# Moving the split rows and split weights of a float32r transformer kernel to other byte offsets

## The chip, the cores and the metric

The kernel runs on one core of one Trainium2 chip. The metric is the device time of one execution in microseconds, the median of the runs; lower is better. Before the change it was 2332.92 us (two runs, 2332.77 to 2333.07).

## What is computed

A two-layer decoder trunk in float32: model width 2048, 16 heads of 128, 256 tokens behind 16 learned prefix tokens (272 positions), feed-forward width 8192.

```python
h = concat([meta, x])                                   # 272 positions
for layer in range(2):
    a = rms_norm(h, norm_attn[layer])
    if layer == 0:
        q, k, v, f_logit = split(a @ fox_w_in)          # 3 * 2048 + 16 columns
        o = forgetting_attention(q, k, v, cumsum(log_sigmoid(f_logit + b)))
        h = h + o @ fox_w_o
    else:
        k, v = split(rms_norm(h, kv_norm) @ w_kv)
        o = stick_breaking_attention(a @ sb_w_q, k, v)
        h = h + o @ sb_w_o
    h = h + square(relu(rms_norm(h, norm_mlp[layer]) @ w_up[layer])) @ w_down[layer]
return rms_norm(h, final_norm)[:, 16:]
```

Every weight is read once: 406 MB over the execution.

## The kernel before

Activations stand feature-major: a tensor of 2048 features is 16 chunks of 128 partitions, each chunk a row of 272 positions (layer 0 and the K/V projection, which need the prefix tokens) or 256 (the rest of layer 1).

For accuracy each float32 operand is split into two float32r parts, hi (the rounded value) and lo (what is left of it). A product of weights and activations is then made of three: hi weights by hi rows, hi weights by lo rows, lo weights by hi rows. They are accumulated in one PSUM bank.

**Rows.** The class `Split` (line 117) holds both parts of an activation tensor in one tile of the pool `xs`, which has two buffers. A chunk has `XROW` = 576 floats of 4 bytes, a pitch of 2,304 bytes or 9 x 256. The hi part begins at float `XHI` = 16 (64 bytes), the lo part right behind it, n floats on, where n is 272 or 256. `self.both` is the two of them as one run of 2n. ScalarE writes the hi part and VectorE the lo part: in `split_chunk` (line 127) after a residual, in `put_split` (line 354) after an attention, and in the MLP's evacuation (lines 496 to 500).

**Weights.** `gemm_group` (line 178) makes 512 output features of one projection, as four accumulators of 128 features. It walks four blocks `kb` of four input chunks each. A block arrives as two `raw` tiles of 128 x 1024 over the SP queue (line 202); of each, ScalarE makes `whi` (line 213) and VectorE `wlo` (line 214), tiles of the pool `wspl` with four buffers for each of the two names. These are [128, 2, 512] floats: two input chunks with a pitch of 2,048 bytes. A load of PE takes 128 of the 512 columns.

**Products.** All of them are issued through `gemm_matmul` on line 172, in an order written out by hand and pinned by dependencies, except in the first group. In layer 0 and the K/V projection (`pairs` false) an input chunk and an accumulator cost three matmuls of 272 columns: hi rows by `whi`, lo rows by `whi`, hi rows by `wlo`. In the rest of layer 1 (`pairs` true) they cost two: `sp.both` by `whi`, 512 columns in one go, so that the two parts land in the two halves of a bank, and hi rows by `wlo`, 256 columns. The evacuation then adds the two halves (`total`, line 254, or two calls of line 252). In the last group of all, accumulator 3 is made with the three separate products (`apart`).

There are 12 groups for Q, K and V of layer 0, 4 for its output projection, 32 for its MLP (4 slices of 4 up and 4 down groups), 4 for the Q of layer 1, 8 for K and V, 4 for its output projection and 32 for its MLP. `uid` numbers them from 1 to 96; the attention between them works on other pools. The order of the pools in memory is `const`, `wraw`, `align` (a pad of 128 bytes), `wspl`, `xs`, `tmp`, `att`.

The labels of the row tiles are `a0` (rows for Q, K, V of layer 0), `o0` (attention output), `m0` (MLP input), `u0_0` to `u0_3` (the four slices of the hidden layer), `a1` (rows for Q of layer 1), `kv` (rows for K and V), `o1`, `m1` and `u1_0` to `u1_3`. The output is collected in `ob`, the last tile of `xs`.

Of the kernel before, what the change touches and what calls it, by code (L numbers as in the profile page):

```python
# [9 lines left out]
F32 = mybir.dt.float32  # L10
F32R = mybir.dt.float32r
# [4 lines left out]
P = 128  # L16
D = 2048
NC = D // P
# [4 lines left out]
BIG = 1.0e30  # L23
QSCALE = 1.0 / math.sqrt(P)
N_FF = 4
XROW = 576
XHI = 16

G_A0, G_M0, G_KV, G_A1, G_M1, G_FIN = range(6)

# [2 lines left out]
def yoco_kernel(ctx: ExitStack, tc: tile.TileContext, hT_in, gains, b_f, w_f, w_qkv0, w_o0, w_up, w_dn,  # L33
                w_kv, w_q1, w_o1, outT):
    nc = tc.nc
# [5 lines left out]
    wspl = ctx.enter_context(tc.tile_pool(name="wspl", bufs=4))  # L41
    xs = ctx.enter_context(tc.tile_pool(name="xs", bufs=2))
# [74 lines left out]
    class Split:  # L117


        def __init__(self, label, t0):  # L120
            n = T - t0
            self.t0 = t0
            rows = xs.tile([P, NC, XROW], F32R, tag="x", name=f"x_{label}")
            self.hi, self.lo = rows[:, :, XHI:XHI + n], rows[:, :, XHI + n:XHI + 2 * n]
            self.both = rows[:, :, XHI:XHI + 2 * n]

    def split_chunk(sp, gi, c):

# [41 lines left out]
    def gemm_matmul(*args, **kw):  # L170

        ins = nc.tensor.matmul(*args, **kw).ins  # L172
        if queued and pinned[0]:
            tc.add_manual_dep(ins, queued[0].name, mybir.DependencyInfo(mybir.DependencyClass.NoSync,
                                                                        mybir.DependencyReason.DATA))
        queued[:] = [ins]

    def gemm_group(wblk, sp, t0, evac, before={}, after={}, load_x=None, pairs=False, apart=()):

        uid[0] += 1
        u = uid[0]
        accs = [pacc.tile([P, 512], F32, tag="acc", name=f"acc_{u}_{m}") for m in range(4)]
        n = T - t0
        for kb in range(4):
            src_w = wblk[kb].rearrange("p (k c) -> p k c", k=4)
            if kb in before:  # L190
                before[kb]()
            piece = 1 if load_x is not None and kb < 2 else 2
            raws = [wraw.tile([P, 2, 512], F32, tag="raw", name=f"raw_{u}_{kb}_{hf}") for hf in range(2)]
            for k0 in range(0, 4, piece):
                if load_x is not None:
                    load_x(range(4 * kb + k0, 4 * kb + k0 + piece))
                if load_x is not None and kb == k0 == 0:

                    for c0 in (0, 256):
                        nc.scalar.dma_start(raws[0][:, 0, c0:c0 + 256], src_w[:, 0, c0:c0 + 256])  # L200
                else:
                    nc.sync.dma_start(raws[k0 // 2][:, k0 % 2:k0 % 2 + piece], src_w[:, k0:k0 + piece])
            parts = []
            for hf in range(2):
                whi = wspl.tile([P, 2, 512], F32R, tag="whi", name=f"whi_{u}_{kb}_{hf}")
                wlo = wspl.tile([P, 2, 512], F32R, tag="wlo", name=f"wlo_{u}_{kb}_{hf}")
                boxes = [(o, piece, 0, 512) for o in range(0, 2, piece)]
                if load_x is not None and kb == hf == 0:
                    boxes[:1] = [(0, 1, 0, 256), (0, 1, 256, 512)]
                for o, no, c0, c1 in boxes:  # L210
                    src = raws[hf][:, o:o + no, c0:c1]
                    hp, lp = whi[:, o:o + no, c0:c1], wlo[:, o:o + no, c0:c1]
                    on_act = nc.scalar.activation(hp, src, AF.Copy)  # L213
                    on_dve = nc.vector.tensor_tensor(out=lp, in0=src, in1=hp.bitcast(F32), op=ALU.subtract)  # L214
                parts.append((whi, wlo))
            if kb in after:
                with tc.issue_after(on_act.ins), tc.issue_after(on_dve.ins):
                    after[kb]()


            if load_x is not None and kb == 0:
                runs = [([kc], range(4)) for kc in range(4)]
            elif kb in (0, 3):
                runs = [(range(4), [m]) for m in range(4)]
            else:
                runs = [(range(2 * hf, 2 * hf + 2), range(4)) for hf in range(2)]
            pinned[0] = load_x is None
            for kcs, ms in runs:
                paired = [m for m in ms if pairs and m not in apart]
                single = [m for m in ms if m not in paired]  # L230
                for kc in kcs:
                    for m in paired:
                        gemm_matmul(accs[m], parts[kc // 2][0][:, kc % 2, m * P:(m + 1) * P], sp.both[:, 4 * kb + kc],
                                    start=kb == kc == 0, stop=False)
                for kc in kcs:
                    for m in paired:
                        gemm_matmul(accs[m][:, :n], parts[kc // 2][1][:, kc % 2, m * P:(m + 1) * P],
                                    sp.hi[:, 4 * kb + kc], start=False, stop=kb == kc == 3)
                for m in single:
                    for kc in kcs:  # L240
                        wh, wl = (w[:, kc % 2, m * P:(m + 1) * P] for w in parts[kc // 2])
                        hi, lo = sp.hi[:, 4 * kb + kc], sp.lo[:, 4 * kb + kc]
                        gemm_matmul(accs[m][:, :n], wh, hi, start=kb == kc == 0, stop=False)
                        gemm_matmul(accs[m][:, :n], wh, lo, start=False, stop=False)
                        gemm_matmul(accs[m][:, :n], wl, hi, start=False, stop=kb == kc == 3)
                if kb == 3:
                    for m in ms:
                        evac(m, [accs[m][:, :n]] + ([accs[m][:, n:]] if m in paired else []))
# [18 lines left out]
    def load_x(chunks):  # L267
        c0, n = chunks[0], len(chunks)
        nc.sync.dma_start(hT[:, c0:c0 + n, :], hT_in[:, c0:c0 + n, :])
        if c0 == 0:  # L270
            nc.sync.dma_start(g_sb, gains)
        for c in chunks:
            split_chunk(xa, G_A0, c)
# [86 lines left out]
    for g in range(4):  # L360
# [11 lines left out]
        if g == 0:  # L372

            gemm_group(w_qkv0[0], xa, 0, lambda m, acc, qT=qT: nc.scalar.copy(qT[:, m, :], acc[0]),
                       after={kb: (lambda kb=kb: first_norm(kb)) for kb in range(4)}, load_x=load_x)
            gate_products()
            box["rstd"] = norm.finish()
            for m in range(4):
                evac_q(m, [qT[:, m, :]])
            forget_gates(box["rstd"])  # L380
        else:
            gemm_group(w_qkv0[3 * g], xa, 0, evac_q)
# [4 lines left out]
        def decays(j):  # L387

            for i, (o, n) in enumerate(((0, 144), (144, T))):
                nc.vector.scalar_tensor_tensor(out=s[:, j, o:o + n], in0=fk[:, j, :n],  # L390
                                               scalar=fq_sb[:, i, 4 * g + j:4 * g + j + 1],
                                               in1=maskA[:, o:o + n], op0=ALU.subtract, op1=ALU.add)

        gemm_group(w_qkv0[3 * g + 1], xa, 0, lambda m, acc: evac_kv(m, acc, kT),
                   after={j: (lambda j=j: decays(j)) for j in range(4)})

# [255 lines left out]
    a, y, t, rs = (fin[:, i, :] for i in range(4))  # L652
# [9 lines left out]
    for i in range(2):  # L662
# [2 lines left out]
            nc.tensor.matmul(pr[:, b * P:(b + 1) * P], rs[:, b:b + 1].to_broadcast([P, P]), ident,  # L665
                             start=True, stop=True)
        prs.append(pr[:, :S])
    ob = xs.tile([P, NC, XROW], F32, tag="x", name="ob")
    pr_sb = tmp.tile([P, T], F32, tag="relu", name="pr_sb")[:, :S]
    nc.scalar.copy(pr_sb, prs[1])  # L670
    for c, n in [(12, 1), (13, 1), (14, 1), (15, 1), (0, 2), (2, 2), (4, 2), (6, 2)]:
# [62 lines left out]
```

## Time and profile before

| | |
|---|---|
| median of the runs | 2332.92 us |
| the profiled execution | 2332.09 us |
| its span, first to last instruction | 2330.3 us |
| mean granted TensorE clock | 0.998 |
| HBM traffic | 407.29 MB read, 176 GB/s over the span |

The profile gives for each engine its busy time and number of instructions. PE is TensorE's matmuls and PEld its weight loads, which overlap them; DVE is VectorE, ACT ScalarE. A line of a group of instructions has the source line, the engine, the operation, output and inputs by their names in the program, the shape, the count, the busy time in us and the mean of one record in ns, and then the idle time in front of them. Records of matmuls overlap, since matmuls are pipelined: two that follow each other are better compared by their starts than by their lengths. The view by stretches gives the busy time of every engine between two points of time.

### The profile page before, as it was taken

The page shows a single profiled execution, that of the slowest core. Times are in us where ns is not written, and L with a number is a line of the kernel's source. Part 1 is how long each engine was busy: PE and PEld are TensorE (multiplying, and loading weights), DVE is VectorE, ACT ScalarE, POOL GpSimd, SP SyncE. Part 2 cuts the span into 40 slices and gives each one's busy share as a digit, 9 for nine tenths or more (in the row PEclk, how much of TensorE's full clock was granted, in tenths as well). Part 3 has the DMA queues.
Part 4 walks back from the last instruction along what each step waited for, and adds up shares of the span by engine and source line. Part 5 has one row for each costly group of instructions (what it writes and reads, how often), then busy time and mean ns, then how long its engine had stood idle before and what let it go on. Part 6 is the DMA issues. An engine that isn't in the chain of part 4 may idle for free.

```text
span 2330.3 us, 39954 instructions
## 1 busy us (share of the span) xinstructions
PE 2319.3 (100%) x16486; PEld 2200.1 (94%) x16486; DVE 1350.6 (58%) x1923; ACT 1064.8 (46%) x1477; POOL 38.9 (2%) x58
## 2 busy tenths in 40 slices
PE   9999999999999999999999999999999999999998
PEld 9999999999999999999998999988888888888887
DVE  7665555654454455445566555566665665655665
ACT  6434344543344344334455444455543543543553
POOL 1000000000000000000000000000000000000000
PEclk9999999999999999999999999999999999999999
DMA  6544545455545555555556444446556556555553
GB/s 233 172 155 163 169 158 171 166 185 173 180 168 185 176 174 180 172 182 172 181 175 198 160 145 145 145 163 199 184 190 198 186 187 199 185 191 195 185 198 128
DMA packets 116630, 412.00 MB, mean 177 GB/s; under 512 B 13264, under 2 KB 16736, under 8 KB 116448
## 3 DMA queue, kind: packets, MB, share of 16 engines
q1 hardware_dynamic: 114560, 406.29, 52.4%
q10 hardware_dynamic: 1888, 3.16, 0.4%
q8 instruction: 129, 2.11, 0.4%
q14 instruction: 53, 0.43, 0.1%
HBM read 407.29 MB, written 2.11 MB: 176 GB/s over the span
## 4 chain that ended last, share of the span: by engine, by line
PE 99%; DVE 0%; ACT 0%; issue 0%; DVEq 0%; ACTq 0%
PE acc L172 96%; PE ps L402 0%; PE pza L581 0%; PE pv L335 0%; PE po L464 0%; PE po L620 0%; PE idle L60 0%; PE pzb L582 0%; PE po L621 0%; PE po L465 0%; PE po L622 0%; DVE ob L676 0%; PE pf L301 0%; PE pf L302 0%; PE pta L597 0%; PE pta L596 0%
## 5 line engine op out<-in xcount | busy, mean ns | idle before, releaser
L214 DVE TENSOR_TENSOR wlo<-raw,whi 128x1024 fp32r<-128x1024 f32 (+1 forms) x773 | 931.7, 1217 | 752.6 <-ACT whi L213 751.7
L213 ACT ACTIVATE whi<-raw 128x1024 fp32r<-128x1024 f32 (+1 forms) x773 | 799.2, 1050 | 960.4 <-PE acc L172 939.9
L172 PE MATMUL acc<-x_u,whi 128*128 128x272 f32 (+2 forms) x3088 | 650.8, 322 | 0.0
L172 PE MATMUL acc<-x_m,whi 128*128 128x272 f32 (+1 forms) x3072 | 649.2, 323 | 0.0
L172 PEld LDWEIGHTS acc<-x_u,whi 128*128 128x128 f32 x3088 | 497.4, 188 | 26.3
L172 PEld LDWEIGHTS acc<-x_m,whi 128*128 128x128 f32 x3072 | 495.5, 188 | 26.9
L172 PE MATMUL acc<-x_u,wlo 128*128 128x272 f32 (+1 forms) x2048 | 441.7, 280 | 0.0
L172 PE MATMUL acc<-x_m,wlo 128*128 128x272 f32 (+1 forms) x2048 | 439.4, 280 | 0.0
L172 PE MATMUL acc<-x_a,whi 128*128 128x272 f32 (+1 forms) x1792 | 363.0, 307 | 0.0
L172 PEld LDWEIGHTS acc<-x_u,wlo 128*128 128x128 f32 x2048 | 339.5, 188 | 15.9
L172 PEld LDWEIGHTS acc<-x_m,wlo 128*128 128x128 f32 x2048 | 338.5, 188 | 16.1
L172 PEld LDWEIGHTS acc<-x_a,whi 128*128 128x128 f32 x1792 | 283.5, 188 | 9.3 <-issue 0.7
L172 PE MATMUL acc<-x_a,wlo 128*128 128x272 f32 (+1 forms) x1024 | 252.9, 284 | 0.0
L172 PE MATMUL acc<-x_kv,whi 128*128 128x272 f32 x1024 | 195.8, 289 | 0.0
L172 PEld LDWEIGHTS acc<-x_a,wlo 128*128 128x128 f32 x1024 | 179.3, 188 | 4.7 <-issue 0.5
L172 PE MATMUL acc<-x_o,whi 128*128 128x272 f32 (+1 forms) x768 | 163.1, 323 | 0.0
L172 PEld LDWEIGHTS acc<-x_kv,whi 128*128 128x128 f32 x1024 | 159.9, 188 | 0.4
L172 PE MATMUL acc<-x_kv,wlo 128*128 128x272 f32 x512 | 145.9, 285 | 0.0
L252 DVE TENSOR_TENSOR hT<-acc,hT 128x256 f32<-128x256 f32 (+1 forms) x239 | 102.5, 429 | 72.0 <-PE acc L172 70.3
L172 PEld LDWEIGHTS acc<-x_o,whi 128*128 128x128 f32 x768 | 124.0, 188 | 6.7
L172 PE MATMUL acc<-x_o,wlo 128*128 128x272 f32 (+1 forms) x512 | 110.8, 282 | 0.0
L172 PEld LDWEIGHTS acc<-x_kv,wlo 128*128 128x128 f32 x512 | 96.2, 188 | 0.1
(226 smaller groups left out, 1038.5 us busy)
## 6 DMA issues: line engine op xcount, KB each, us to landing
raw<-w_up SPq DMA_DIRECT2D x256, 512.0 KB, 4.7
raw<-w_dn SPq DMA_DIRECT2D x256, 512.0 KB, 4.8
raw<-w_qkv SPq DMA_DIRECT2D x92, 512.0 KB, 4.1
raw<-w_o SPq DMA_DIRECT2D x64, 512.0 KB, 4.5
raw<-w_kv SPq DMA_DIRECT2D x64, 512.0 KB, 3.9
raw<-w_q SPq DMA_DIRECT2D x32, 512.0 KB, 4.7
fk<-f_dram ACTq DMA_DIRECT2D x4, 544.0 KB, 5.4
raw<-w_qkv SPq DMA_DIRECT2D x7, 256.0 KB, 4.7
```

Of the source, the lines that this page charges most:

```text
L172: ins = nc.tensor.matmul(*args, **kw).ins
L213: on_act = nc.scalar.activation(hp, src, AF.Copy)
L214: on_dve = nc.vector.tensor_tensor(out=lp, in0=src, in1=hp.bitcast(F32), op=ALU.subtract)
L252: nc.vector.tensor_tensor(out=hT[:, c, t0:], in0=a, in1=hT[:, c, t0:], op=ALU.add)
```

## The change

Four things are moved, and nothing is computed otherwise.

Each row tile gets a pitch and two starts of its own, from a table `ROWS` (pitch, hi, lo, in floats). In layer 0 the pitch is 640 floats and hi and lo lie 320 floats (5 x 256 bytes) apart, so that both start at the same place modulo 256 bytes: 192 for `a0`, 160 for `kv`, 176 for `o0`, 208 for `m0`, and 224, 240, 200 and 216 for `u0_0` to `u0_3`. In layer 1 `a1` stays as it was; `u1_0`, `u1_1` and `u1_2` start at 80, 96 and 48 bytes, still in one run; `o1` (hi at 0, lo at 64 modulo 256), `m1` (hi at 64, lo at 0) and `u1_3` (hi at 192, lo at 0) lie in two pieces with a gap between them, and in the last two lo comes first in memory.

`self.both` becomes a view of two runs of n with the gap left out. Where lo comes first, the products of hi rows by `wlo` go to the upper half of the bank, where the hi part's products are.

The tiles of `whi` and `wlo` grow from 512 to 576 floats per chunk, and the 512 in use start 0, 16, 32 or 48 floats on, by the group's number modulo 4.

The larger tiles need 12,800 bytes more per partition; `dynamic_dma_scratch_size=1024` makes the room.

```diff
-XROW = 576
-XHI = 16
+
+ROWS = {"a0": (640, 48, 368), "kv": (640, 40, 360), "o0": (640, 44, 364), "m0": (640, 52, 372), "u0_0": (640, 56, 376),
+        "u0_1": (640, 60, 380), "u0_2": (640, 50, 370), "u0_3": (640, 54, 374),
+        "a1": (576, 16, 272), "o1": (576, 0, 272), "m1": (576, 272, 0), "u1_0": (576, 20, 276), "u1_1": (576, 24, 280),
+        "u1_2": (576, 12, 268), "u1_3": (640, 304, 0)}
+XROW = 640
+
+WOFF = (0, 16, 32, 48)
...
-            rows = xs.tile([P, NC, XROW], F32R, tag="x", name=f"x_{label}")
-            self.hi, self.lo = rows[:, :, XHI:XHI + n], rows[:, :, XHI + n:XHI + 2 * n]
-            self.both = rows[:, :, XHI:XHI + 2 * n]
+            rows = xs.tile([P, NC * XROW + 64], F32R, tag="x", name=f"x_{label}")
+            pitch, hi, lo = ROWS[label]
+            o = min(hi, lo)
+            rows = rows[:, o:o + NC * pitch].rearrange("p (c t) -> p c t", c=NC)
+            self.hi, self.lo = (rows[:, :, k - o:k - o + n] for k in (hi, lo))
+
+            d = abs(lo - hi)
+            self.both = rows[:, :, :2 * d].rearrange("p c (i t) -> p c i t", i=2)[:, :, :, :n]
+            self.low_first = lo < hi
...
-                whi = wspl.tile([P, 2, 512], F32R, tag="whi", name=f"whi_{u}_{kb}_{hf}")
-                wlo = wspl.tile([P, 2, 512], F32R, tag="wlo", name=f"wlo_{u}_{kb}_{hf}")
+                o = WOFF[u % 4]
+                whi = wspl.tile([P, 2, 576], F32R, tag="whi", name=f"whi_{u}_{kb}_{hf}")[:, :, o:o + 512]
+                wlo = wspl.tile([P, 2, 576], F32R, tag="wlo", name=f"wlo_{u}_{kb}_{hf}")[:, :, o:o + 512]
...
-                        gemm_matmul(accs[m][:, :n], parts[kc // 2][1][:, kc % 2, m * P:(m + 1) * P],
+                        gemm_matmul(accs[m][:, n:] if sp.low_first else accs[m][:, :n],
+                                    parts[kc // 2][1][:, kc % 2, m * P:(m + 1) * P],
                                     sp.hi[:, 4 * kb + kc], start=False, stop=kb == kc == 3)
...
-    ob = xs.tile([P, NC, XROW], F32, tag="x", name="ob")
+    ob = xs.tile([P, NC * XROW + 64], F32, tag="x", name="ob")[:, :NC * XROW].rearrange("p (c t) -> p c t", c=NC)
...
-    nc = bacc.Bacc("TRN2", target_bir_lowering=False, num_devices=1)
+    nc = bacc.Bacc("TRN2", target_bir_lowering=False, num_devices=1, dynamic_dma_scratch_size=1024)
```

## The prediction

> **What bounds the kernel now.** I read the page first: its busy times and its chain of waits.
>
> ```profile
> span 2330.3 us, 39954 instructions
> ...
> PE 2319.3 (100%) x16486; PEld 2200.1 (94%) x16486; DVE 1350.6 (58%) x1923; ACT 1064.8 (46%) x1477; POOL 38.9 (2%) x58
> ...
> PE 99%; DVE 0%; ACT 0%; issue 0%; DVEq 0%; ACTq 0%
> ```
>
> PE never rests, and 99% of the chain is its own work; the page puts 96% on line 172, the products of `gemm_group`. All that PE ever waited for, by the list of waits, is 1.3, 1.1 and 0.2 us. So only the pace of the products on line 172 can move the time; what DVE, ACT and the DMAs gain or lose lies beside them. Next I read that pace, from the timeline of PE, first in the MLP of layer 0 and then in that of layer 1 (start, length, operation, count):
>
> ```profile
> 599.76 0.41 PE L172 MATMUL acc<-x_u,whi 128*128 128x272 f32 x2
> 600.01 0.28 PE L172 MATMUL acc<-x_u,wlo 128*128 128x272 f32 x1
> 600.13 0.41 PE L172 MATMUL acc<-x_u,whi 128*128 128x272 f32 x2
> ...
> 605.73 0.41 PE L172 MATMUL acc<-x_u,whi 128*128 128x272 f32 x2
> ```
>
> ```profile
> 1717.29 1.07 PE L172 MATMUL acc<-x_u,whi 128*128 128x512 f32 x4
> 1718.20 0.63 PE L172 MATMUL acc<-x_u,wlo 128*128 128x256 f32 x4
> 1718.67 1.09 PE L172 MATMUL acc<-x_u,whi 128*128 128x512 f32 x4
> 1719.60 0.62 PE L172 MATMUL acc<-x_u,wlo 128*128 128x256 f32 x4
> 1720.06 1.07 PE L172 MATMUL acc<-x_u,whi 128*128 128x512 f32 x4
> ```
>
> Starts count here, since records overlap. From 599.76 to 605.73 lie 16 triples (hi and lo rows against `whi`, hi rows against `wlo`): 5.97/16 = 373 ns each. Within one, the two `whi` products take 0.25 us together and the third 0.12. In layer 1 eight pairs take 1720.06 - 1717.29 = 2.77 us: 346 ns a pair, 230 for 512 columns and 116 for 256.
>
> The same difference shows in the means of one record, by shape:
>
> ```profile
> L172 PE MATMUL acc<-x_m,whi 128*128 128x272 f32 x2048 | 382.7, 288 | 0.0
> ...
> L172 PE MATMUL acc<-x_m,wlo 128*128 128x272 f32 x1024 | 289.8, 283 | 0.0
> ...
> L172 PE MATMUL acc<-x_m,whi 128*128 128x512 f32 x1024 | 266.5, 392 | 0.0
> ...
> L597 PE MATMUL pta<-el,ntri_r 128*128 128x512 f32 x8 | 3.2, 395 | 0.0
> ```
>
> Two line through layer 1's two sizes: 256 columns more cost 230 - 116 = 114 ns, 0.445 ns a column; 272 columns would then start 116 + 7 = 123 ns apart. The third product of a triple, at 121, is on that line, the first two, at 126, about 5 above it. The records say the same: 288 against 283.
>
> Counts, from the code: layer 0 and the K/V projection have 56 groups of 64 triples, 3,584; layer 1 has 40 groups of 64 pairs, 2,560. 3,584 x 373 ns = 1,337 us and 2,560 x 346 ns = 886 us: 2,223 of 2,330.3. Each ns on a triple is 3.6 us of the kernel, each ns on a pair 2.6.
>
> **The change part by part.** It adds no product, removes none, and moves bytes alone, so it is priced in ns per product.
>
> *Rows of layer 0.* Now hi starts at 64 bytes and lo, right behind it, at 64 + 1,088 = 1,152, which is 128 modulo 256. After, both start at one place modulo 256 (320 floats apart), between 160 and 240 by label. Trace shows no layer-0 product at these places, so I bound it by the two paces above: all three as the third, 3 x 121 = 363 (-10 ns, -36 us); all three as the first two, 3 x 126 = 378 (+5 ns, +18 us). Which? The first group is in another order: four hi in succession at one start, four lo, four hi against `wlo`.
>
> ```profile
> 8.78 1.17 PE L172 MATMUL acc<-x_a,whi 128*128 128x272 f32 x8
> 9.78 0.67 PE L172 MATMUL acc<-x_a,wlo 128*128 128x272 f32 x4
> ...
> 13.31 0.29 PE L172 MATMUL acc<-x_a,whi 128*128 128x272 f32 x1
> ```
>
> From 8.78 to 13.31 there are 36 products: 126 ns each, though most follow one at their own start. The last four of each twelve take 0.50 to 0.51 us, 126 each, where a `wlo` product in a triple takes 121. So an equal start alone doesn't give 121, and I take 0 with both ends kept.
>
> *Rows of layer 1.* `a1` stays; `u1_0`, `u1_1`, `u1_2` move by 16 to 32 bytes (bounded below); `o1`, `m1`, `u1_3` are read in two runs of 256. Nearest row: L597 reads its 512 columns in two runs with a gap, at 395 against 392: +3 ns. That falls on 256 + 1,024 + 240 = 1,520 products of 512: +4 us, taken. The ends: -3 ns and +3 ns on all 2,560, -8 and +8 us. The `low_first` address on line 237 costs nothing: same count, same bank. It leaves the evacuation alone, which adds both halves anyway.
>
> *Weights displaced.* Three groups in four load from a start 64, 128 or 192 bytes on: 0.75 x 15,888 = 11,916 loads. The means of one load by shape:
>
> ```profile
> L172 PEld LDWEIGHTS acc<-x_m,whi 128*128 128x128 f32 x3072 | 495.5, 188 | 26.9
> ...
> L582 PEld LDWEIGHTS pzb<-qT,kT 128*128 128x128 f32 x32 | 6.1, 190 | 0.8
> L597 PEld LDWEIGHTS pta<-el,ntri_r 128*128 128x128 f32 x8 | 1.5, 188 | 0.0
> ```
>
> Loads of 128 columns take 188 to 190 from `wspl`, `att` and `const` alike, tiles with other starts and pitches. I take 0. What the load doesn't show is a meeting of its reads with the rows'. Bounds: the 5 to 6 ns by which two equal products differ, either way, on 11,916: -65 to +65 us.
>
> In the Trainium skill, SBUF — State Buffer (Who interferes with whom) says that PE has one read port for the moving operand and an independent one for weights, and never waits on anyone. By that rule this part, and the displacement with it, is worth 0. The trace agrees as far as the other engines go: in the stretch from 8.78 ACT is busy 4.53 of 4.53 us and DVE 4.43, and a product takes 126 ns against 124 in the stretch at 600 (DVE 2.71 of 5.97). No row separates the two ports.
>
> *ACT and DVE* write the parts with a row pitch of 576 instead of 512: 8 + 8 instructions a group at 1.05 and 1.22 us, about 10 us of a group's 24 on DVE. Hidden under PE; if each cost 10% more, DVE would hold 62% of the span instead of 58. The scratch reserve and the larger tiles issue nothing.
>
> Sum: 2,332.1 (the profiled execution, 2,330.3 of span and 1.8 around it) + 0 + 4 + 0 = 2,336. The median shown is 0.8 higher: 2,337.
>
> **The rivals.** *The step goes* (hi and lo at one place are the point): triples at 363, -36 us, plus 4: 2,301. For: the two `whi` products differ from the third in where the next row starts. Against: the first group. 0.18.
>
> *The excess goes too.* The Trainium skill, TensorE: Matmul & The Clock Gate (Back-to-back issue gap), gives N / 2.4 + 2.5 ns: by it an estimate of 348 a triple and 325 a pair, and 2,333 - 90 - 54 = 2,189. From rows alone: if the start of a row were what makes 512 columns cost 230, a gain as large as layer 1's possible 8 us and layer 0's 36, plus the 65 of the weights, would give 2,333 - 109 = 2,224. For: nothing but the regular 5 ns step, which proves that place matters somewhere. Against: two starts and three sizes lie within 5 ns of one line. 0.12.
>
> *Slower: the displaced weights meet the rows.* Weights start at multiples of 256 within their tiles now, rows at 64 or 128. With four displacements every distance occurs. If three in four lose the 6 ns that the third product now saves, 11,916 x 6 = 71 us: 2,404. It passes 2% (47 us) from 3.9 ns per product. For: PE's loader in layer 0 is busy without a gap, 425.00 of 425.00 us between 715 and 1140, so a longer load has no cover there. Against: 188 everywhere. 0.24, of which 0.17 beyond 2%.
>
> *Not what it says:* rows cut from a flat tile could be ordered as one piece, and a down projection would wait for the last chunk of its rows. After the last up product at 648.1 the last x_u is written at 651.6: 3.5 us at 10 such places, 35 us: 2,368. 0.06.
>
> **How the numbers follow.** Forecast, little moves: 0.40, 2,310 to 2,352. Faster by over 2% (about what a measurement of this kernel tells from no change) is below 2,286: the excess case and a little of the first rival, 0.14. Slower, above 2,380: 0.18. Within: 0.68. For 8 in 10 I leave out the lower half of the excess case and the far end of the meeting weights: 2,270 to 2,400.
>
> **What would show it.** Right: triples near 373 and pairs near 346 ns under every label, DVE and ACT the same. The first rival: `whi` records at 283 in layer 0. The weights: four groups in succession with four paces, and the pace back at groups with displacement 0. The ordering: PE idle by 3 us at the turn from up to down. The forecast is wrong if one label's triples move by over 10 ns.

## The result, and the profile after

The changed kernel takes 2357.98 us (two runs, 2357.78 and 2358.17) against 2332.92: a ratio of 1.0108, 95% interval [1.0088, 1.0128]. It is slower by 25 us, inside the range of the prediction and short of 2%. The profiled execution took 2358.17 us.

The page of the changed kernel, its busy times and the chain by engine:

```profile
span 2356.4 us, 39954 instructions
...
PE 2345.3 (100%) x16486; PEld 2218.1 (94%) x16486; DVE 1350.8 (57%) x1923; ACT 1064.6 (45%) x1477; POOL 37.7 (2%) x58
...
PE 99%; DVE 0%; DMA 0%; ACT 0%; issue 0%; SPq 0%; DVEq 0%; ACTq 0%
```

The number of instructions is the same on every engine. PE is busy for 26.0 us more and the span is 26.1 us longer; DVE and ACT are where they were. The list of PE's waits names one that is new, of 0.4 us, in the first group. So next to nothing waits: the same matmuls start further apart. Which ones, the stretches show. These are 22 us out of each of the four groups of `u0_0` (rows at 224), whose weights are displaced by 64, 128, 192 and 0 bytes in this order; behind each engine's busy time stands the number of its instructions:

```profile
534.00:556.00 22.00, 22.00 (x180) 22.00 (x179) 11.28 (x13) 8.12 (x10) 0.00 (x0) 1.00 0.55 188
558.00:580.00 22.00, 22.00 (x178) 22.00 (x177) 10.20 (x11) 6.59 (x7) 0.00 (x0) 1.00 0.54 187
582.00:604.00 22.00, 22.00 (x177) 22.00 (x177) 10.14 (x11) 6.64 (x7) 0.00 (x0) 1.00 0.55 185
606.00:628.00 22.00, 22.00 (x176) 22.00 (x176) 10.16 (x10) 6.78 (x7) 0.00 (x0) 1.00 0.54 184
```

In equal time PE gets through 180, 178, 177 and 176 products, at the full granted clock (the 1.00). What the change makes different between these four groups is the place of the weights alone. From the starts in the trace, averaged over a group and without the gaps that other products make, a triple takes 370, 376, 377 and 380 ns here, where it took 373 in each of the four before. In the same way the eight products of 512 and eight of 256 columns that follow each other in the timeline of `m1`'s first group (displacement 64):

```profile
1631.04 2.08 PE L184 MATMUL acc<-x_m,whi 128*128 128x512 f32 x8
1632.96 1.12 PE L184 MATMUL acc<-x_m,wlo 128*128 128x256 f32 x8
1633.92 0.59 PE L165 MATMUL pms_m<-ssq_m,mean_w 128*128 128x256 f32 x2
```

and in its second (displacement 128):

```profile
1654.29 2.03 PE L184 MATMUL acc<-x_m,whi 128*128 128x512 f32 x8
1656.16 1.10 PE L184 MATMUL acc<-x_m,wlo 128*128 128x256 f32 x8
1657.10 2.03 PE L184 MATMUL acc<-x_m,whi 128*128 128x512 f32 x8
```

The first is 2.88 / 8 = 360 ns a pair, the second 2.81 / 8 = 351, against 345 to 346 before. Over all groups a triple went from 373.5 to 376.2 ns and a pair from 345.4 to 350.8: with 64 units a group, 9.7 us for the triples and 13.8 us for the pairs, 23.5 of the 26.1. Another 2.2 us are lost before the second group starts, at 36.0 us instead of 33.8; over the kernels below that start lies anywhere from 33.7 to 37.5.

The records by shape, and one of the loads:

```profile
L184 PE MATMUL acc<-x_m,whi 128*128 128x272 f32 x2048 | 384.8, 288 | 0.0
...
L184 PE MATMUL acc<-x_m,wlo 128*128 128x272 f32 x1024 | 295.1, 288 | 0.0
L184 PE MATMUL acc<-x_m,whi 128*128 128x512 f32 x1024 | 270.9, 396 | 0.0
```

```profile
L184 PEld LDWEIGHTS acc<-x_m,whi 128*128 128x128 f32 x3072 | 501.6, 189 | 29.0
```

The step of 5 ns between the `whi` and the `wlo` products of layer 0 is gone, but upwards: 288 and 288, where it was 288 and 283 before. The record of a load says 189 where it said 188, although between the four groups of a label it is the place of the weights that moved the pace.

### The profile page after: what moved, and what is told of

It is laid out like the page before. It is cut to its first block, busy times and chain, and to the rows that moved or that the text cites. A ratio compares the mean times of both kernels' runs of the same rounds, so it can differ in the third digit from the quotient of the medians.

```text
span 2356.4 us, 39954 instructions
## 1 busy us (share of the span) xinstructions
PE 2345.3 (100%) x16486; PEld 2218.1 (94%) x16486; DVE 1350.8 (57%) x1923; ACT 1064.6 (45%) x1477; POOL 37.7 (2%) x58
## 4 chain that ended last, share of the span: by engine, by line
PE 99%; DVE 0%; DMA 0%; ACT 0%; issue 0%; SPq 0%; DVEq 0%; ACTq 0%
PE acc L184 95%; PE ps L416 0%; PE pza L595 0%; PE pv L349 0%; PE po L478 0%; PE po L634 0%; DMA raw<-w_qkv 0%; PE pzb L596 0%; PE po L635 0%; PE po L479 0%; PE po L636 0%; DVE ob L690 0%; DVE wlo L227 0%; PE pf L316 0%; PE pf L315 0%
## 5 line engine op out<-in xcount | busy, mean ns | idle before, releaser
L184 PE MATMUL acc<-x_u,whi 128*128 128x272 f32 (+2 forms) x3088 | 657.8, 323 | 0.0
L184 PEld LDWEIGHTS acc<-x_u,whi 128*128 128x128 f32 x3088 | 503.3, 188 | 27.9
L184 PEld LDWEIGHTS acc<-x_m,whi 128*128 128x128 f32 x3072 | 501.6, 189 | 29.0
L184 PE MATMUL acc<-x_u,wlo 128*128 128x272 f32 (+1 forms) x2048 | 449.9, 285 | 0.0
L184 PE MATMUL acc<-x_m,wlo 128*128 128x272 f32 (+1 forms) x2048 | 447.3, 284 | 0.0
L184 PEld LDWEIGHTS acc<-x_m,wlo 128*128 128x128 f32 x2048 | 341.6, 189 | 17.4
L184 PEld LDWEIGHTS acc<-x_u,wlo 128*128 128x128 f32 x2048 | 341.6, 188 | 16.9
```

## The experiments

The theory (A): the pace depends on the distance between the start of the weights that are being loaded and the start of the rows that are being streamed, modulo 256 bytes. Its rivals: the place of the rows alone (B), the place of the weights alone (C). Below, a distance is row start minus weight start, taken within the tiles; where hi and lo differ it is that of hi. Paces are averages over a group or label from the starts in the trace, as above. Groups that run with 272 columns are counted with layer 0, the K/V projection (`kv`) among them.

### Each half of the change alone

Weights displaced, rows as before the change, alike in all labels of a layer (`e1_weights_only`):

```diff
+ROWS = {"a0": (576, 16, 288),
...
+        "a1": (576, 16, 272),
...
 WOFF = (0, 16, 32, 48)
```

> Rows where they were before the change (64, and lo right behind hi), weights displaced by 0, 64, 128, 192 in turn. Theory A, the pace hangs on the distance between the start of the weights and that of the rows: the four displacements give four paces, alike in every fourth group; in layer 1 the four groups of a1, whose rows the change left alone, already show them, 346, 350, 347 and 351 ns a pair for 0, 64, 128, 192 against 346 before, so layer 1 loses about 2 ns a pair, 5 us; layer 0 moves by up to 3 ns a triple either way; 2330 to 2350 us, and 373 and 345 ns in the groups with displacement 0. Theory B, the place of the rows alone: 2333 us and no group differs from before. Theory C, the place of the weights alone: about 2358, as with the whole change.

2349.01 us, ratio 1.0068 [1.0055, 1.0082]: +16 us. In the four groups of `u0_0`, displaced by 64, 128, 192 and 0:

```profile
532.00:554.00 22.00, 22.00 (x177) 22.00 (x176) 10.88 (x12) 7.99 (x10) 0.00 (x0) 1.00 0.57 184
556.00:578.00 22.00, 22.00 (x179) 22.00 (x178) 10.37 (x11) 6.89 (x7) 0.00 (x0) 1.00 0.55 186
580.00:602.00 22.00, 22.00 (x176) 22.00 (x176) 10.17 (x10) 6.80 (x7) 0.00 (x0) 1.00 0.55 184
604.00:626.00 22.00, 22.00 (x179) 22.00 (x178) 10.46 (x11) 7.06 (x7) 0.00 (x0) 1.00 0.54 182
```

Two of the four groups are slow, two as before: 377.4, 373.3, 379.6 and 373.3 ns a triple. This repeats in every label of layer 0, but for `kv` and most groups of `a0`, where both slow ones stand at 377. In layer 1 it is 350.0, 346.9, 351.3 and 345.8 a pair, in `m1` and `u1` as in `a1`. B falls: the rows didn't move. Layer 0 lost up to 6 ns a triple where 3 were expected.

ScalarE and VectorE write the parts of the weights, so they too write to other places here. Their writes are not what slows PE: in the groups with displacement 192 from `m0` to `u0_3`, `whi` products that run while both engines are idle start 126.4 ns apart and those that run while both are busy 126.1, the `wlo` products 127.4 and 125.8.

Rows moved, all weights at 0 (`e2_rows_only`):

```diff
-WOFF = (0, 16, 32, 48)
+WOFF = (0, 0, 0, 0)
```

> Rows as in the change, all weights at displacement 0. Theory A: every group has the pace that the changed kernel's groups with displacement 0 have: per product of 272 columns 123.4 for a0 and kv, 126.7 for o0, m0, u0_0, u0_2, 125 for u0_1, 127.2 for u0_3, against 124.5 before, which sums to +10 us; in layer 1 +0 (a1), +6 (o1), +4.5 (m1), +5 to +8 (u1) ns a pair, +12 us; together 2356. Theory B: 2358, as with the whole change, with the four groups of a label alike at their mean. Theory C: 2333.

2353.62 us, ratio 1.009 [1.0076, 1.0103]: +20 us, 2.4 below what A summed to. C falls. Nearly all labels have the pace that the changed kernel's undisplaced groups had: 370 ns a triple for `a0` and `kv`, 380 for `m0`, `u0_0` and `u0_2`, 375 for `u0_1`, 382 for `u0_3`. One doesn't: `o0` stands at 370, where the changed kernel's one undisplaced `o0` group has 380. The halves cost 16 and 20 us and together 25, so they don't add up, as with a distance they need not.

### Both shifted by the same amount

Rows and weights 64 bytes on (`e4_both_shifted`):

```diff
+ROWS = {"a0": (576, 32, 304),
...
+        "a1": (576, 32, 288),
...
+WOFF = (16, 16, 16, 16)
```

> Rows and weights both 64 bytes on, so that every distance between them is that of before. Theory A in its pure form (distance alone): 373 ns a triple and 345 a pair, 2333 us. Theory B or C (a place modulo 256 of its own counts): other paces, anywhere between 2320 and 2360; the groups of a1 and kv in the changed kernel suggest a few ns.

2334.62 us, ratio 1.0008 [0.9998, 1.0017]. The four groups of `u0_0`, all displaced by 64:

```profile
533.00:555.00 22.00, 22.00 (x179) 22.00 (x178) 11.14 (x12) 8.26 (x8) 0.00 (x0) 1.00 0.51 169
557.00:579.00 22.00, 22.00 (x179) 22.00 (x178) 11.20 (x12) 8.27 (x8) 0.00 (x0) 1.00 0.51 170
581.00:603.00 22.00, 22.00 (x179) 22.00 (x178) 11.21 (x12) 8.26 (x8) 0.00 (x0) 1.00 0.50 168
605.00:627.00 22.00, 22.00 (x179) 22.00 (x178) 11.20 (x12) 8.26 (x8) 0.00 (x0) 1.00 0.49 168
```

Every layer-0 label is at 373.3 to 373.9 ns a triple, layer 1 at 346.2 to 346.5 a pair. The same displacement of 64 that cost 4 ns a triple with the rows in place costs nothing when the rows go along. Even the step within a triple is back: in `u0_0` the two `whi` products take 126.2 ns each and the third 121.0, as before the change, where the displacement alone had made all three 125.8. So what counts is where weights and rows lie to each other. Only this one shift was tried.

### Sixteen distances

Rows of layer 0 at 192, of layer 1 at 64, weights in steps of 16 bytes by the group's number modulo 16 (`e5_scan16`):

```diff
+WOFF = (0, 4, 8, 12, 16, 20, 24, 28, 32, 36, 40, 44, 48, 52, 56, 60)
```

> hi and lo rows of layer 0 at 192, rows of layer 1 at 64 as before, and the weights of the groups displaced in steps of 16 bytes, 0 to 240, by the group's number modulo 16. Theory A (the distance row start minus weight start, modulo 256, sets the pace): the layer-0 groups repeat the paces found so far at equal distance, in ns a triple: 370 at 192 and 160, 370 to 380 at 176, 373 at 144, 380 at 128, 208 and 64, 375 to 377 at 96, 80, 48, 32, 0 and 240; layer 1: 346 at 64 and 347 at 192, 350 at 0, 351 at 128. A best place below 368 or below 344 would be a version to build. If the place of the rows counts instead, all layer-0 groups stand at 370. Some 2340 to 2350 us in all.

2356.93 us (one run), 7 above the time named. The layer-0 groups range from 370 to 380 ns with the rows in one place throughout. At 192 and 160 they have 370, at 128, 208 and 64 380, at 240 375, at 0 376, and at 48 and 32 377, all as expected. Three distances missed: 144 has 380, not 373, and 96 and 80, for which 375 to 377 was expected, have 380 in most labels (377 in `a0` and `kv` at 80, 376 in `kv` at 96). Distances 176 and 112 have more than one pace over the runs, between 370 and 380; at 112 this run alone has both, 370 in `a0` and `u0` and 380 in `kv`. In layer 1, 346 to 347 at 64 and 192, 348 to 354 elsewhere. No place beats 370 and 345. So the distance takes part, but the distance modulo 256 does not fix the pace by itself, and what else does is not known.

### Shorter loads

All but the first and last product of an accumulator load 64 columns of weights instead of 128 (`e6_half_loads`), then 32 (`e9_quarter_loads`), on top of `e1_weights_only`; the columns left out are left out of the projections:

```diff
-gemm_matmul(accs[m][:, :n], wh, lo, start=False, stop=False)
+gemm_matmul(accs[m][:64, :n], wh[:, :64], lo, start=False, stop=False)
```

> Rows as before the change, weights displaced by 0, 64, 128, 192 in turn, and all but the first and last product of a group's accumulator load 64 columns of weights instead of 128, so that half of each projection is left out. If the reads of the loads meet those of the rows (theory A), a load has half as many reads and the differences between the four displacements, 373.3, 377.4, 373.3 and 379.7 ns a triple in layer 0 and 346, 350, 347, 351 ns a pair in layer 1, shrink to half or less, and the whole gets nearer to 370 and 341. If only where a row and a load begin counts (rival), the four paces stay within 1 ns of these.

2326.13 us. Neither number came out. In `u0_0`, the displacements of 64, 128, 192 and 0 stand at 373.4, 367.1, 373.2 and 370.7 ns a triple, in layer 1 at 346.1, 350.2, 348.1 and 341.6 a pair. The differences didn't shrink (6.3 and 8.6 ns); but nor did the paces stay. The best pace of layer 0 fell by 6 ns, and in layer 1 displacement 128 went from second best to worst. So the length of the load takes part, and not only where it begins.

> As e6_half_loads with 32 columns of weights per load, so that three quarters of each projection are left out. From 128 to 64 columns the mean over the four displacements fell from 375.9 to 371.0 ns a triple and from 348.5 to 346.5 a pair. If the loads' reads cost the rows' reads time (theory A), it falls again, by about half as much, to 367 to 369 and 345 to 346, and the four displacements come nearer together (3 ns). If the loads cost nothing and only their start shifts the rows, the means stay at 371 and 346.5 within 1 ns.

2333.16 us. In the four groups of `u0_0`, displaced as above:

```profile
528.00:550.00 22.00, 22.00 (x179) 19.21 (x177) 11.20 (x13) 8.31 (x11) 0.00 (x0) 1.00 0.55 182
552.00:574.00 22.00, 22.00 (x179) 19.18 (x177) 10.37 (x12) 6.97 (x7) 0.00 (x0) 1.00 0.56 183
575.00:597.00 22.00, 22.00 (x179) 19.25 (x178) 10.76 (x11) 7.87 (x8) 0.00 (x0) 1.00 0.55 172
600.00:622.00 22.00, 22.00 (x179) 19.17 (x178) 10.37 (x11) 6.77 (x7) 0.00 (x0) 1.00 0.57 184
```

179 four times: 373.4, 373.4, 373.7 and 373.4 ns a triple, and 346.1 to 347.1 a pair, with the weights as displaced as in `e1_weights_only`. With short loads the place of the weights no longer counts for the whole of a triple; within it the third product still varies, from 122.6 to 126.6 ns. ScalarE and VectorE write to the displaced places as much as before. So the place acts through the loads; but a product with a 32-column load also fills only 32 of the 128 partitions of its bank, and the two were not separated. The other half of the expectation missed: the mean of layer 0 didn't fall on but rose, to 373.5, and that of layer 1 stayed, at 346.6. In layer 0 the products run at just the pace of the kernel before. Its 373 may then be what rows at 64 and 128 cost by themselves, which no run shows directly. Long loads at a bad distance add to it, and with these rows none went below it; half loads did, to 367 and 371. Why was not tried, nor were short loads with the rows at 192, where long loads have 370.

### What ran before, and the lo rows alone

`e8_history` puts all layer-0 rows at distance 176, with every second group of half the stages at 192, to see whether the two paces at 176 hang on the group in front:

```diff
+WOFF = (4, 4, 4, 4, 4, 4, 4, 4, 4, 0, 4, 0, 4, 0, 4, 0)
```

> Rows of layer 0 at 192, weights at 16 bytes in all groups, but at 0 in every second group of half of the stages. Distance 176 had 370 ns a triple in one kernel and 380 in two others. Theory H (at some distances two paces hold themselves, and which one depends on what ran before): groups at 16 bytes behind a group at 0 (370) and groups at 16 behind groups at 16 differ, or all stand at 380 with changes that keep within a stage. Theory P (the distance alone, with a place of its own for some): all groups at 16 bytes have one pace, 380, those at 0 have 370; about 2345 us.

2354.97 us, 10 above the 2345; layer 1, whose weights moved along, went to 348.5 ns a pair. The first group aside, all 41 groups at 176 have 380 ns and all 14 at 192 have 370, behind either kind. So here it isn't the neighbouring group; the two paces at one distance (370 for rows at 176 and weights at 0 in `e2_rows_only`, 380 for the same in the changed kernel) stay unexplained.

`e10_lo_scan` keeps hi where it is best and moves lo alone:

```diff
+ROWS = {"a0": (640, 48, 320), "kv": (640, 48, 328), "o0": (640, 48, 336),
...
+        "a1": (640, 16, 272), "o1": (640, 16, 280), "m1": (640, 16, 288),
...
+WOFF = (0, 0, 0, 0)
```

> Weights at displacement 0 in tiles as before; hi rows of layer 0 at 192 and of layer 1 at 64, lo rows a further 0 to 224 bytes on (modulo 256), another step in each label. Theory A: each product's pace goes with its own distance, so only the products of lo rows move: in layer 0 a third of a triple, 370 at lo = hi (u0_2, u0_3) and up to 377 where lo stands at a distance of 64, 128 or 208; in layer 1 the pairs stay within 346 to 351. If the step from one row to the next is what counts (the third product's 121 before the change), some label in layer 0 gets below 368 or in layer 1 below 345: a version to build.

2355.36 us. With lo where hi is, 370; 64 to 224 bytes from it, 373 to 380. `kv` and `m0`, at 379 and 380, lie beyond the 377 that a third of a triple could explain, so a displaced lo row slows its neighbours too; and `u0_1`, whose lo row lies at 160, a distance that had 370, has 377. In layer 1, 346 with lo right behind hi (`a1`), 347.5 to 352 otherwise. None is faster.

### A version that beats both

All layer-0 rows at 192, layer 1 as before the change, weights at 0 in tiles of 576 floats (`e3_rows_192`):

```diff
+ROWS = {"a0": (640, 48, 368),
...
+        "a1": (576, 16, 272),
...
+WOFF = (0, 0, 0, 0)
```

> A candidate: hi and lo of every layer-0 label at 192 modulo 256, layer 1 and weights as before the change. Theory A: all triples of layer 0 at the 123.4 ns per product that a0 has at displacement 0, against 124.5: 10,752 x 1.05 = -11 us, 2322. Theory B with the mean of a0 (125.5 over its four displacements): +11 us, 2344. If the label and not the place makes a0's pace: o0, m0 and u0 stay near 126 and the time near 2345.

2322.92 us, ratio 0.9958 [0.9945, 0.997]: -10 us where A said -11. The timeline in the MLP of layer 0:

```profile
600.07 0.41 PE L181 MATMUL acc<-x_u,whi 128*128 128x272 f32 x2
600.31 0.28 PE L181 MATMUL acc<-x_u,wlo 128*128 128x272 f32 x1
...
607.83 0.41 PE L181 MATMUL acc<-x_u,whi 128*128 128x272 f32 x2
```

21 triples in 7.76 us are 370 ns each, in every label. Layer 1 stands at 346.3 a pair, 1.1 above the kernel before. `e7_rows_192_pitch512` asked whether the pitch of the weights makes that:

```diff
-whi = wspl.tile([P, 2, 576], F32R, tag="whi", name=f"whi_{u}_{kb}_{hf}")[:, :, o:o + 512]
+whi = wspl.tile([P, 2, 512], F32R, tag="whi", name=f"whi_{u}_{kb}_{hf}")
```

> As e3_rows_192, but with the weight tiles of before, 512 floats per chunk instead of 576. e3 had 346.3 ns a pair in layer 1 where the kernel before had 345.2: if the pitch of the weights makes that, layer 1 is back at 345.2, 2,560 x 1.1 = 2.8 us, and the time 2320; layer 0 stays at 370 ns a triple. If it does not, 2323.

2323.52 us, ratio 0.9958 [0.9942, 0.9975]: no, 346.3 again. Layer 0 has the same 370 too, although the two chunks of a weight tile now lie 2,048 bytes apart instead of 2,304, which bears out that a step of 256 changes nothing. In the kernel before, `a1` has 346.4 as well and the labels after it 345.2; what lets it fall there is open, and worth 2.4 us. With its distances kept, `e4_both_shifted` doesn't have that fall either, so up to 2.4 us of what the other variants lose in layer 1 may not be due to their offsets.

## Why the prediction was right, and where it was not

The time lies in the range and within 2%, the likeliest of the three, but the forecast case, "little moves", did not happen: 2358 is beyond its own 2,310 to 2,352, and the sign is that of the third rival. The range held because it left room for that rival; the terms of the forecast, 0 + 4 + 0 against a measured 25 us, did not hold. Nor did its sign of being right: triples and pairs did not stay near 373 and 346. Its sign of being wrong, one label's triples off by over 10 ns, did not come either: the worst label, `u0_2`, moved by 8, though one of its groups moved by 13, to 386.5.

**What bounds the kernel** held: the pace of the line of the products moved the time. DVE, ACT and the DMAs gave no part of the 25 us but what lies in the 2.2 us at the start. ACT and DVE were to be hidden with their new pitch; their busy times didn't even change.

**Weights displaced, "I take 0"**: this step failed. It rested on a load's record, 188 to 190 ns from every tile, and the record went to 189 while the pace moved by up to 6 ns a triple with the rows in place. (Nor is that record the same everywhere: the loads of 128 columns in the transposes take 138 to 148 ns.) With the rows in place the displacement alone cost 16 us: 8.1 in layer 0 and 7.9 in layer 1, where up to 2.4 may not be due to the offsets. The third rival, the weights meeting the rows, named this mechanism, and the runs with equal shift and with short loads bear it out; its size was too large. It put 6 ns on 11,916 products, 71 us. The whole 16 us on as many are 1.3 ns each, because some displacements are as good as none (128 in layer 0) and because 6 ns is the loss of a whole triple at the worst. Its sign, the pace back in groups with displacement 0, showed only with the rows in place: in the changed kernel these groups have up to 382.

The rule of the Trainium skill, SBUF — State Buffer (Who interferes with whom), by which PE's two read ports are independent and this part is worth 0, is not borne out: weights displaced alone cost 0.68%, and PE's new wait in that run is 0.4 us. That PE is not held up by what ScalarE and VectorE write remains, by the 126.4 and 126.1 ns above.

**Rows of layer 0**: 0 taken, with -36 and +18 us as ends; alone they measured +8.0, inside. The better half of the reasoning was the first group's: an equal start of hi and lo didn't give 121 ns per product. It evened all three out, at 123 to 127 by distance. So the first rival's step did go, yet not to its 363 a triple: 370 at the best place, and worth 10 us in all. (That four hi rows and then four lo rows come in succession in the first group was an assumption: the trace names the tile of the rows, not the part.)

**Rows of layer 1**: +4 taken, +-8 as ends; alone they measured +11.7, above the end, even without those 2.4. The bound came from one row in two runs, 395 against 392, and took 3 ns as the most that a place could cost. The worst label, `u1_1`, lost 8 ns a pair, and `m1` at displacement 64 in the whole change 14.

**The excess** did not go in any run: with full-length loads no label was under 370 a triple and 345 a pair. The estimates worked out from the Trainium skill, TensorE: Matmul & The Clock Gate (Back-to-back issue gap), were 348 and 325, and no run here comes near them. **The ordering** rival fell: PE has no new wait at any turn from up to down.

## What to carry to other kernels

Where TensorE is busy throughout with float32r products, the start of the moving rows and that of the weights are a tuning knob: 1.1% was lost here and 0.4% gained. Choose them together, since moving either alone can undo a good pair. Read the pace from the starts of successive matmuls, group by group, not from record lengths. One kernel with another offset in each group maps sixteen places at once, but a good place has to be confirmed in a kernel that uses it throughout, since one distance had two paces here. An equal length of the load's records is no evidence that a load is free.

## What had not been expected of the hardware

The mean pace of products of one shape repeats to some 0.2 ns from group to group and comes in few values (in layer 0 mostly 370, 373, 375, 377 and 380 ns a triple). Full loads at a good distance are not the floor (these loads leave out part of the projections): loads of 64 columns gave 367 and 341.6, loads of 32 columns 373 and 346 to 347, so a shorter load is not always the cheaper one.
